# Small loads of rope tables and lambdas on POOL's queue, and another spread of the late modulation chunks

## The chip, the cores and the metric

The kernel runs on one core of a Trainium2 chip. The metric is the time of one execution on the device, in microseconds, as the median of several runs. Five engines of the core are named as in the profile: PE (matrix products; PEld is its weight load), DVE (vector), ACT (activations and copies), POOL (GpSimd) and SP (which here only issues DMAs). SPq, POOLq and so on are the engines' own instruction queues: they work in program order, and an instruction that waits holds what is queued behind it on the same engine.

## The reference, cut to what matters

One layer over 256 latent tokens and 256 context tokens of width 2048, all in fp32. A conditioning vector gives six modulation vectors of 2048 values. Attention and pooling run side by side, are merged by gates and projected; an MLP follows.

```python
mod = (jax.nn.silu(c) @ w_mod[l] + b_mod[l])[:, None, :]
sa, ca, ga, sm, cm, gm = jnp.split(mod, 6, axis=-1)
...
h_c = modulate(x_ctx, norm_attn_w[l], sa_c, ca_c)          # context: keys and values only
h = modulate(x, norm_attn_w[l], sa, ca)
p = h @ w_in[l]
q = axial_rope(rmsnorm(split_qk(p[..., Q_OFF:K_OFF]), q_norm_w[l]), row, col)
k = axial_rope(rmsnorm(split_qk(p[..., K_OFF:V_OFF]), k_norm_w[l]), row, col)
...
mix = token_mixer(q, k_all, v_all, p[..., P_OFF:G_OFF], p[..., G_OFF:], lam, ...)
x = x + ga * mix
x = x + gm * sq_relu_mlp(modulate(x, norm_mlp_w[l], sm, cm), w_ff1[l], w_ff2[l])
```

`token_mixer` holds a differential attention (8 heads, each the softmax of one pair of queries and keys minus `lam` times that of another), a pooling of the tokens in four groups with windows of 2, 4, 8 and 16, two up-projections, two sigmoid gates and the projection by `w_o`. `lam` is made from four small vectors, the lambdas. `ga`, `cm`, `sm` and `gm` are not needed before the projection and the MLP.

## The kernel before, in words

**The work.** All weights are fp32 in DRAM. They come in chunks of 128 x 1024 (512 KB), each into a tile `raw`. ACT casts a chunk to a high part `whi` (L245), DVE subtracts for a low part `wlo` (L246), and PE makes each product from high x high, high x low and low x high (`mm3`, L275 to 278; L454, L455 and L460 for the wide groups; L1028 and L1031 in the MLP). The high x low and high x high products come first, those with `wlo` last.

**The stages.** In order: the modulation of the attention norm (`w_m`, 16 steps f of 4 chunks, PE's `mod`) mixed with the first keys and queries; first values; second queries; second keys; second values; pooling (`w_p`, four groups); the gates and up-projections (`w_gb_in`, `w_b`, `w_ga_in`, `w_a`, four rounds); the projection (`w_o`); the MLP. Attention's scores run beside the second queries to the pooling: PE makes a block of scores, DVE its maximum (L687), ACT the exponential with the sum (L691), DVE the reciprocal and the factors (L694, L695, L697). ACT's exponential is the last reader of the scores' PSUM bank.

**Loads.** The list `stream` (from L127) names every load in its order, and SP issues them in this order a few chunks ahead of use (`load_next`, `wchunk` L255). Among the first loads stand two entries `prq`, at step 9 and step 11 of the modulation: three DMAs with rope tables and lambdas into tabs, wkt and wqt, then one more with the second pair of lambdas into a part of wqt. The last one overwrites columns that DVE still reads for the first pair of lambdas, so it waits for DVE. All four are issued in line L206.

**Late chunks.** `ga`, `cm`, `sm` and `gm` aren't made by PE. Each entry of `stream` has a `rate`, which its load adds to a credit (L248); each whole credit advances the generator `late_gen` (L597) by one. A vector has two halves, and a half takes 17 advances: one that clears the accumulator on POOL (L613) and loads the bias row (L614), and 16 that each issue the load of one chunk on SP and, one or two ticks later, one multiply-add on DVE over 128 x 1024 (`late_part`, L625). Behind the 16th of a half `late_fold` adds up the 128 partitions: seven DMAs that accumulate 64, 32, 16, 8, 4, 2 and 1 partitions onto the ones below (L630), all on POOL's queue, each waiting until the one before has landed; then one DMA to a row (L635; for `cm` L638 to L641) and one that spreads the row over the partitions (L642). Instructions that are not pinned (`pin`) are put in order on each engine by the language's scheduler, so that a clearing, a bias row or an addition on POOL can stand some way off its written place. The order of the names is fixed, so the rates decide in which stage the chunks of each lie.

**POOL's other work** around the change: for each group of pooling, `za` is cleared at its ends (L778, L779), ACT copies the PSUM into it (L780), POOL adds shifted copies (L785), and DVE finishes it (L796, L798, L800; `pool_diff` is placed some ticks later). For attention's norm POOL clamps the squares (L721) which PE sums (L725). In the MLP POOL squares the relu (L1039), ACT casts that (L272), and PE needs it for the next product.

Of the kernel before, what the change touches and what calls it, by code (L numbers as in the profile page):

```python
# [38 lines left out]
PRQ = {}  # L39
# [9 lines left out]
def layer(ctx: ExitStack, tc, a, out):  # L49
    nc = tc.nc  # L50
# [24 lines left out]
    def work(name, shape=None, dt=F32):  # L75
        return pool.tile(shape or [P, 512], dt, tag="w2", name=name, bufs=9)

    def s16(name, shape, dt=F32):
        return pool.tile(shape, dt, tag="s16", name=name, bufs=7)

    def s8(name, shape, dt=F32):
        return pool.tile(shape, dt, tag="s8", name=name, bufs=2)
# [32 lines left out]
    def raw_chunk(src, n=1024):  # L115
        raw = pool.tile([P, n], F32, tag="raw", name="raw", bufs=6)
        sp.dma_start(raw, src)
        return raw
# [9 lines left out]
    def plan(name, *idx, rate=0.0):  # L128
        stream.append(((name,) + idx, rate))
# [12 lines left out]
            plan("w_k", 0, f // 2)  # L142
            plan("w_q", 0, f // 2)
    FIRST_LOADS = len(stream)
    for n, g, rate in (("w_v", 0, 0.75), ("w_q", 1, 1.0), ("w_k", 1, 1.5), ("w_v", 1, 1.5)):
        for ch in range(8):
            plan(n, g, ch, rate=0.0 if (n, g) == ("w_v", 1) and ch < 3 else rate)
    for g in range(4):
        for i in range(4):
            plan("w_p", 2 * g + i // 2, i % 2, rate=0.5)  # L150
            if g > 1 and i == 1:
                plan("pool_w", g - 2)
    for g in range(4):
        for n, nk in (("w_gb_in", 8), ("w_b", 4), ("w_ga_in", 8), ("w_a", 4)):
            for ch in range(nk):
                plan(n, g, ch, rate=0.6)
                if g == 0 and n == "w_gb_in" and ch in (1, 7):
                    plan("pool_w", 2 if ch == 1 else 3)
    for g in range(4):
        for ch in range(8):  # L160
            plan("w_o", g, ch, rate=0.5 if g < 2 else 0.0)
            if ch % 4 == 0:
                plan("x", ch // 4, g)
    for b in range(9):
# [15 lines left out]
    def x1_tile():  # L180
        if not x1s:
            x1s.append(s16("x1", [P, 2, D]))
        return x1s[0]
# [5 lines left out]
    def mod_raw(f, i):  # L189

        home = f % 2 if f > 7 else f % 4
        if home == 0:
            return pool.tile([P, 1024], F32, tag="raw", name="raw", bufs=6)
        n = 2 if home == 1 else 4
        if i % n == 0:
            wide[0] = (s8 if home == 1 else s16)("raw", [P, n, 1024])
        return wide[0][:, i % n, :]

    def load_next():
        key, rate = stream[len(loaded)]  # L200
        src = a[key[0]]
        for i in key[1:] if key[0] != "prq" else ():
            src = src[i]
        if key[0] == "prq":
            for dst, names in prq[key[1]]:
                nc.sync.dma_start(dst, a["prq"][:, PRQ[names[0]][0]:PRQ[names[-1]][1]])  # L206
            loaded.append((key, None, None))
            return
        if key[0] in ("cT", "x"):
            dst = cT[:, 4 * key[1]:4 * key[1] + 4, :] if key[0] == "cT" else x1_tile()[:, key[1], key[2] * 512:key[2] * 512 + 512]  # L210
            nc.sync.dma_start(dst, src)
            loaded.append((key, None, None))
            return
        n = src.shape[-1]
        if key[0] == "w_m":
            raw = mod_raw(*key[1:])
            sp.dma_start(raw, src)
            loaded.append((key, raw, raw))
            return
        if key[0] in ("w_k", "w_q") and key[1] == 0:  # L220
            raw = pool.tile([P, n], F32, tag="aT", name="raw", bufs=2)
            sp.dma_start(raw, src)
            loaded.append((key, raw, raw))
            return
        raw = raw_chunk(src, n)
        if key == ("w_ff1a", 0):
            hi, lo = (pool.tile([P, n], F32R, tag="aT", name=nm, bufs=2) for nm in ("hi0", "lo0"))
        elif key == ("w_o", 3, 4):
            pair = s8("pair", [P, 2, 1024], F32R)
            hi, lo = pair[:, 0, :], pair[:, 1, :]  # L230
        elif key in (("w_ff1a", 2), ("w_ff1a", 3)):
            i = 2 * (key[1] - 2)
            if i == 0:
                early.append(s16("early", [P, 4, 1024], F32R))
            hi, lo = early[0][:, i, :], early[0][:, i + 1, :]
        elif key == ("w_ff1a", 1):
            halves = [[work(nm, dt=F32R) for nm in ("hi1", "lo1")] for _ in range(2)]
            for h in range(2):
                split(*halves[h], raw[:, h * 512:h * 512 + 512])
            loaded.append((key, *zip(*halves)))  # L240
            return
        else:
            hi = pool.tile([P, n], F32R, tag="whi", name="whi", bufs=3)
            lo = pool.tile([P, n], F32R, tag="wlo", name="wlo", bufs=3)
        act.copy(hi, raw)  # L245
        vec.tensor_sub(lo, raw, hi.bitcast(F32))  # L246
        loaded.append((key, hi, lo))
        credit[0] += rate if late[0] is not None else 0.0  # L248
        credit_rate[0] = rate
        while credit[0] >= 1.0:  # L250
            credit[0] -= 1.0
            if "gm" not in mods or mods["gm"] is not None or key[0] in ("w_ff1a", "w_ff1"):
                next(late[0], None)

    def wchunk(*key, ahead=AHEAD):  # L255
        while len(loaded) < min(done[0] + 1 + ahead, len(stream)) or loaded[done[0]][1] is None:
            if loaded and done[0] < len(loaded) and loaded[done[0]][1] is None:
                done[0] += 1
                continue
            load_next()  # L260
        got, hi, lo = loaded[done[0]]
        assert got == key, (got, key)
        loaded[done[0]] = None
        done[0] += 1
        tick()
        return hi, lo
# [4 lines left out]
    def split(hi, lo, src):  # L271
        act.copy(hi, src)  # L272
        vec.tensor_sub(lo, src, hi.bitcast(F32))
# [26 lines left out]
    def pr(name):  # L300
# [30 lines left out]
    prq = (((tabs[:, 2:4], ("cos", "sin")), (wkt, ("wk",)), (wqt, ("wq", "lq1", "lk1"))),  # L331
           ((wqt[:, 1:3], ("lq2", "lk2")),))
# [846 lines left out]
```

## Time and profile before

| | us |
|---|---|
| median of 3 runs | 1462.01 |
| lowest and highest run | 1460.66, 1462.44 |
| profiled execution, its own time | 1463.71 |
| its span | 1461.9 |
| mean granted clock of PE in it | 0.996 of full speed |

One execution was taken by the profiler, and all durations and waits come from it. A row of the timeline has the start in us, the duration (of several alike in a row: to the end of the last one), engine, line, operation, output and inputs, the count, and in brackets the idle time before it with what ended it. A row of the waits has the engine with the line that waited, the line and engine waited for, the total in us, how often, and the longest. A row of the windows has the stretch and its length, the busy time of PE, PEld, DVE, ACT and POOL with counts, and then the granted clock of PE, the share of the DMA engines' time, and GB/s. In the group of DMA issues a row ends in the size in KB and the us from issue to landing.

### The profile page before, as it was taken

What the parts mean: (1) busy time and instruction counts of PE and PEld (TensorE: products, weight loads), DVE (VectorE), ACT (ScalarE), POOL (GpSimd) and SP (SyncE); (2) the same over time, 40 slices, a digit from 0 to 9 for tenths busy, and PEclk for the clock granted to TensorE, in tenths of its full rate; (3) what the DMA queues carried; (4) which work ended last, traced back from release to release, by engine and by line L of the source; (5) the groups of instructions that cost most, each with busy time, mean ns of one, the idle gap of its engine ahead of it and who ended that gap; (6) DMA issues with size and microseconds to landing.
All of it is one profiled execution on the core that took longest, in us unless ns stands there. A gap on an engine that the chain in (4) does not pass through costs nothing.

```text
span 1461.9 us, 19786 instructions
## 1 busy us (share of the span) xinstructions
PE 1436.2 (98%) x7448; PEld 1182.0 (81%) x7448; DVE 990.7 (68%) x1218; ACT 669.3 (46%) x901; POOL 172.8 (12%) x194
## 2 busy tenths in 40 slices
PE   6999999999999999999999999999999999999998
PEld 4667887778888888888888888888888888888887
DVE  4557796858887777777767656666666465555675
ACT  5225335456654444444545545445344354544432
POOL 0001111104401010100001000011000110000260
PEclk9999999999999999999999999999999999999999
DMA  9997595445689999999746777787776665565563
GB/s 374 409 366 280 191 316 183 145 125 167 213 299 322 324 302 321 304 339 298 224 162 208 231 244 232 237 248 248 242 242 235 204 216 189 190 196 189 187 196 122
DMA packets 101328, 355.22 MB, mean 243 GB/s; under 512 B 12928, under 2 KB 13952, under 8 KB 101232
## 3 DMA queue, kind: packets, MB, share of 16 engines
q1 hardware_dynamic: 97200, 345.52, 69.5%
q0 software_dynamic: 4032, 8.44, 2.6%
q8 instruction: 58, 0.95, 0.3%
q14 instruction: 38, 0.31, 0.1%
HBM read 347.61 MB, written 2.13 MB: 239 GB/s over the span
## 4 chain that ended last, share of the span: by engine, by line
PE 84%; DMA 9%; DVE 4%; issue 1%; ACT 1%; POOL 0%; SPq 0%; DVEq 0%; ACTq 0%; POOLq 0%
PE f L1028 13%; PE f L455 8%; PE f L454 8%; PE f L460 8%; PE f L1031 7%; PE pg L454 4%; PE pg L455 4%; PE pg L460 4%; DMA raw<-in_w_m_dram 4%; DMA gm_bc<-gm_bc 2%; PE pyy L454 2%; PE pyy L455 2%; PE pyy L460 2%; PE wo L455 2%; PE wo L460 2%; PE wo L454 2%
## 5 line engine op out<-in xcount | busy, mean ns | idle before, releaser
L246 DVE TENSOR_TENSOR wlo<-raw,whi 128x1024 fp32r<-128x1024 f32 (+1 forms) x430 | 535.5, 1248 | 329.3 <-ACT whi L245 304.7
L245 ACT CAST whi<-raw 128x1024 fp32r<-128x1024 f32 (+1 forms) x430 | 449.8, 1048 | 547.2 <-PE f L455 184.5
L1028 PE MATMUL f<-h,whi 128*128 128x512 f32 x896 | 224.4, 393 | 1.0 <-ACT whi L245 1.0
L454 PE MATMUL f<-whi,act 128*128 128x512 f32 x512 | 199.4, 390 | 0.0
L455 PE MATMUL f<-whi,act 128*128 128x512 f32 x512 | 199.4, 389 | 0.0
L1028 PEld LDWEIGHTS f<-h,whi 128*128 128x128 f32 x896 | 161.7, 189 | 30.2 <-ACT whi L245 1.2
L460 PE MATMUL f<-wlo,act 128*128 128x512 f32 x512 | 136.9, 389 | 0.0
L1031 PEld LDWEIGHTS f<-h,wlo 128*128 128x128 f32 x896 | 122.3, 191 | 8.7
L1031 PE MATMUL f<-h,wlo 128*128 128x256 f32 x896 | 124.9, 283 | 0.0
L460 PEld LDWEIGHTS f<-wlo,act 128*128 128x128 f32 x512 | 96.1, 188 | 19.9
L454 PEld LDWEIGHTS f<-whi,act 128*128 128x128 f32 x512 | 96.1, 188 | 19.8
L455 PEld LDWEIGHTS f<-whi,act 128*128 128x128 f32 x512 | 96.2, 188 | 19.6
L454 PE MATMUL pg<-whi,hL 128*128 128x512 f32 x256 | 100.8, 394 | 0.0
L455 PE MATMUL pg<-whi,hL 128*128 128x512 f32 x256 | 99.7, 390 | 0.0
L625 DVE SCALAR_TENSOR_TENSOR sb<-raw,sil,sb 128x1024 f32<-128x1024 f32 x64 | 83.0, 1297 | 1.8 <-DMA sb<-in_b_cm_dram 1.8
L1039 POOL TENSOR_TENSOR rsq<-relu 128x512 f32<-128x512 f32 x28 | 29.2, 1042 | 427.3 <-ACT relu L1038 417.1
L460 PE MATMUL pg<-wlo,hL 128*128 128x512 f32 x256 | 68.5, 390 | 0.0
L454 PEld LDWEIGHTS pg<-whi,hL 128*128 128x128 f32 x256 | 48.1, 188 | 10.2 <-issue 0.2
L455 PEld LDWEIGHTS pg<-whi,hL 128*128 128x128 f32 x256 | 48.1, 188 | 10.0 <-issue 0.2
L460 PEld LDWEIGHTS pg<-wlo,hL 128*128 128x128 f32 x256 | 48.1, 188 | 10.0
L630 POOL DMA_DIRECT2D sb<-sb x28 | 22.4, 798 | 243.2 <-DVE sb L625 129.6
L1053 DVE TENSOR_TENSOR acc<-f,acc 128x512 f32<-128x512 f32 x48 | 30.9, 686 | 20.4 <-PE f L460 20.4
(280 smaller groups left out, 2185.4 us busy)
## 6 DMA issues: line engine op xcount, KB each, us to landing
raw<-in_w_ff_dram SPq DMA_DIRECT2D x240, 512.0 KB, 4.2
raw<-in_w_m_dram SPq DMA_DIRECT2D x64, 512.0 KB, 10.2
raw<-in_w_ga_dram SPq DMA_DIRECT2D x32, 512.0 KB, 4.6
raw<-in_w_cm_dram SPq DMA_DIRECT2D x32, 512.0 KB, 5.1
raw<-in_w_gb_in_dram SPq DMA_DIRECT2D x32, 512.0 KB, 4.7
raw<-in_w_ga_in_dram SPq DMA_DIRECT2D x32, 512.0 KB, 4.9
raw<-in_w_sm_dram SPq DMA_DIRECT2D x32, 512.0 KB, 5.4
raw<-in_w_o_dram SPq DMA_DIRECT2D x32, 512.0 KB, 4.7
```

The source lines that it names most:

```text
L245: act.copy(hi, raw)
L246: vec.tensor_sub(lo, raw, hi.bitcast(F32))
L454: pe.matmul(banks[t], tok(h, k, 0, tt), wt, start=k == 0, stop=False)
L455: pe.matmul(banks[t], tok(h, k, 1, tt), wt, start=False, stop=False)
L460: pe.matmul(banks[t], tok(h, k, 0, tt), wt, start=False, stop=k == 2 * nk - 1)
L625: pin(vec.scalar_tensor_tensor(o, raw, sil[:, 0, k:k + 1], o, ALU.mult, ALU.add))
L630: nc.gpsimd.dma_start(o[0:n, :], o[n:2 * n, :], accum_op=ALU.add)
L1028: pe.matmul(ps, hi[:, kk * P:kk * P + P], both(h2, k), start=k == 0, stop=False)
L1031: pe.matmul(ps[:, T:2 * T], lo[:, kk * P:kk * P + P], act_slice(h2, k, 0), start=False, stop=k == KT - 1)
L1039: gp.tensor_mul(sq, r, r)
L1053: vec.tensor_add(acc[:, t, gs], bs[t], acc[:, t, gs])
```

## The change

The four DMAs of line L206 are issued on POOL's queue. And the rates differ in six groups of loads: lower in second keys and second values, higher in pooling, gates and projection.

```diff
     FIRST_LOADS = len(stream)
-    for n, g, rate in (("w_v", 0, 0.75), ("w_q", 1, 1.0), ("w_k", 1, 1.5), ("w_v", 1, 1.5)):
+    for n, g, rate in (("w_v", 0, 0.75), ("w_q", 1, 1.0), ("w_k", 1, 1.0), ("w_v", 1, 0.75)):
         for ch in range(8):
             plan(n, g, ch, rate=0.0 if (n, g) == ("w_v", 1) and ch < 3 else rate)
     for g in range(4):
         for i in range(4):
-            plan("w_p", 2 * g + i // 2, i % 2, rate=0.5)
+            plan("w_p", 2 * g + i // 2, i % 2, rate=0.6)
...
             for ch in range(nk):
-                plan(n, g, ch, rate=0.6)
+                plan(n, g, ch, rate=0.63)
...
-            plan("w_o", g, ch, rate=0.5 if g < 2 else 0.0)
+            plan("w_o", g, ch, rate=0.6 if g < 2 else 0.0)
...
             for dst, names in prq[key[1]]:
-                nc.sync.dma_start(dst, a["prq"][:, PRQ[names[0]][0]:PRQ[names[-1]][1]])
+                nc.gpsimd.dma_start(dst, a["prq"][:, PRQ[names[0]][0]:PRQ[names[-1]][1]])
```

How the order of the instructions differs is shown at three places. An `x2` stands for two alike in a row.

On SP, in the modulation of the attention norm (before with −, after with +):

```order
-L217 DMA raw<-in_w_m_dram 128x1024
-L206 DMA tabs<-in_prq_dram 128x256
-L206 DMA wkt<-in_prq_dram 128x64
-L206 DMA wqt<-in_prq_dram 128x192
-L217 DMA raw<-in_w_m_dram 128x1024 x7
-L222 DMA raw<-in_w_k_dram 128x1024
-L222 DMA raw<-in_w_q_dram 128x1024
-L217 DMA raw<-in_w_m_dram 128x1024
-L206 DMA wqt<-in_prq_dram 128x128
-L217 DMA raw<-in_w_m_dram 128x1024 x7
```

The four L206 are gone from SP. They are now the first DMAs on POOL's queue, ahead of the first L613 (the clearing of ga_bc).

On DVE, in second values, between the last rope step L487 of the second keys and the next maxima L687; before:

```order
L694 RECIPROCAL rs<-sm_2344 128x2
L625 SCALAR_TENSOR_TENSOR ga_bc<-raw,sil,ga_bc 128x1024
L487 TENSOR_TENSOR qraw<-qraw,wkt 128x512
L695 TENSOR_TENSOR rs<-rs,lam_89 128x1
L246 TENSOR_TENSOR wlo<-raw,whi 128x1024
L697 SCALAR_TENSOR_TENSOR e<-e,rs 128x512
L625 SCALAR_TENSOR_TENSOR ga_bc<-raw,sil,ga_bc 128x1024 x2
L246 TENSOR_TENSOR wlo<-raw,whi 128x1024
L687 TENSOR_REDUCE mx<-sc 128x1 x2
```

And at the same place on DVE after the change:

```order
L694 RECIPROCAL rs<-sm_2331 128x2
L487 TENSOR_TENSOR qraw<-qraw,wkt 128x512
L695 TENSOR_TENSOR rs<-rs,lam_89 128x1
L246 TENSOR_TENSOR wlo<-raw,whi 128x1024
L697 SCALAR_TENSOR_TENSOR e<-e,rs 128x512
L246 TENSOR_TENSOR wlo<-raw,whi 128x1024
L687 TENSOR_REDUCE mx<-sc 128x1 x2
```

Three multiply-adds of late chunks are gone from this place; one stands behind the maxima, as before.

On POOL, from the second clearing of za for the last group of pooling to its additions; before:

```order
L785 TENSOR_TENSOR za<-za 128x265 x2
L778 MEMSET za 128x8
L779 MEMSET za 128x8
L778 MEMSET za 128x8
L779 MEMSET za 128x8
L785 TENSOR_TENSOR za<-za 128x271
L785 TENSOR_TENSOR za<-za 128x269
```

And on POOL after the change, from the accumulators of the next vector (sb), which are now cleared ahead of the third group's additions, to the clamp L721:

```order
L613 MEMSET sb 128x1024 x2
L785 TENSOR_TENSOR za<-za 128x271 x2
...
L614 DMA sb<-in_b_sm_dram 1x16x64
L630 DMA ga_bc<-ga_bc 64x1024
L614 DMA sb<-in_b_sm_dram 1x16x64
L630 DMA ga_bc<-ga_bc 32x1024
L630 DMA ga_bc<-ga_bc 16x1024
...
L630 DMA ga_bc<-ga_bc 8x1024
L785 TENSOR_TENSOR za<-za 128x271 x2
L785 TENSOR_TENSOR za<-za 128x269 x2
```

The fold of ga's second half, which stood ahead of the first group's additions, now stands around those of the last group: its first four DMAs ahead of the eight additions, three behind them, and then the clamp L721. The fold of sm's second half moves back in the same way, by some five chunks of the projection's loads.

## The prediction

> **What bounds the kernel now.** I read the page first, then the waits of PE, the waits of SP's DMA queue, the granted clock around the longest waits, and then the timeline of each place that the change touches. The profiled execution took 1463.7 us: the span below and 1.8 us around it. It is 1.7 us above the median of the three runs (1462.0). I work out a difference in the profiled execution and add it to the median.
>
> ```profile
> span 1461.9 us, 19786 instructions
> PE 1436.2 (98%) x7448; PEld 1182.0 (81%) x7448; DVE 990.7 (68%) x1218; ACT 669.3 (46%) x901; POOL 172.8 (12%) x194
> PE 84%; DMA 9%; DVE 4%; issue 1%; ACT 1%; POOL 0%; SPq 0%; DVEq 0%; ACTq 0%; POOLq 0%
> ```
>
> PE is the bound: busy for 98%, and 84% of the chain that ended last. An edit can only win back PE's idle time, or time at a lower clock; it loses what new idle time it makes. PE's waits, longest first:
>
> ```profile
> PE ssq L68 <- DVE sq L68: 10.6, 3, 6.9
> PE mod L68 <- DMA raw<-in_w_m_dram: 4.0, 6, 1.1
> PE qkT L492 <- ACT e L691: 2.6, 1, 2.6
> PE pin L278 <- DVE wlo L246: 1.3, 2, 1.0
> PE f L1028 <- ACT whi L245: 1.0, 1, 1.0
> ```
>
> The first row is the norm of the inputs and is not touched. The second and third are where the two parts of the change reach PE. Gates and projection are absent from the list: there PE waits for nothing that lasts. The clock fell in a stretch of 3.4 us right behind the second and the third wait:
>
> ```profile
> 97.40:100.80 3.40, 3.40 (x12) 2.72 (x9) 0.45 (x1) 0.00 (x0) 0.00 (x0) 0.50 1.03 420
> 278.30:281.70 3.40, 3.40 (x11) 2.76 (x10) 1.44 (x4) 1.73 (x5) 0.00 (x0) 0.51 0.87 287
> ```
>
> The last three columns are clock, DMA share and GB/s. Half clock for 3.4 us costs PE 1.7 us each time.
>
> **Part one, the rope tables and lambdas leave SP.** Four small DMAs leave SP's queue. Only the last of them waits: it overwrites columns of wqt that DVE still has to read.
>
> ```profile
> SPq L206 <- DVE wqt L68: 8.1, 1, 8.1
> ```
>
> ```profile
> 80.65 0.33 SPq L217 DMA_DIRECT2D raw<-in_w_m_dram  x1
> ```
>
> ```profile
> 89.66 0.33 SPq L206 DMA_DIRECT2D wqt<-in_prq_dram  x1
> 90.04 3.66 SPq L217 DMA_DIRECT2D raw<-in_w_m_dram  x7
> ```
>
> ```profile
> 95.11 0.64 PE L68 MATMUL mod<-raw,cv 128*32 128x256 f32 x8 [0.63 <-DMA raw<-in_w_m_dram]
> 96.86 0.64 PE L68 MATMUL mod<-raw,cv 128*32 128x256 f32 x8 [1.12 <-DMA raw<-in_w_m_dram]
> ```
>
> ```profile
> raw<-in_w_m_dram SPq DMA_DIRECT2D x64, 512.0 KB, 10.2
> ```
>
> SP issues nothing between 80.65 and 89.66. A load of this stage lands 10.2 us after its issue, so the one of 80.65 lands near 90.9, and in an unbroken train a load of 512 KB follows every 1.3 us (at the 420 GB/s above): the second at 93.5, the third at 94.8. PE, which has waited for them, starts on the second behind the stall at 95.11 and on the third at 96.86. The hole is 1.6 to 2.1 us, and PE shows it as 0.63 + 1.12 = 1.75. On POOL, the waiting DMA stands ahead of the memsets of ga_bc, more than 30 us later in the program, so nothing is held up there. The three that don't wait go to the very front of POOL's queue: the same 0.26 MB beside the first loads instead of beside later ones, a move of 0.7 us (0.26 MB at some 374 GB/s) that pays back later; I put it at nothing, and at most at 0.7 us lost. If only the hole goes, 1.7 us are won. If the half clock goes with it, 1.75 + 1.7 = 3.4 us could be, but then PE comes up against the train of loads, which itself moves by only 1.6 to 2.1 us. I take 2.6, the middle of the ends 1.7 and 3.4, since both rows count.
>
> The Trainium skill, "DMA: Bandwidth & Descriptors", section "Issuing engines are not separate DMA queues", speaks against this part: DMAs of all engines end on the same 16 DMA engines, and issuing on another one only saves issue time, which is small. By it this part is worth the 0.33 us of an issue row, and the sum below would be 2.3 us higher. The rows above show more than an issue: a wait in order that holds seven other loads; that is a rival below.
>
> **Part two, fewer late chunks in second keys and values.** Up to the end of second values the credits fall from 33.5 (8 × 0.75 + 8 × 1 + 8 × 1.5 + 5 × 1.5) to 25.75 (the last two now 8 × 1 and 5 × 0.75). Some eight late chunks move from there to pooling (8 to 9.6 credits), gates (57.6 to 60.5) and projection (8 to 9.6). In the DVE order shown in the section on the change, three multiply-adds L625 vanish between L694 and the pair L687.
>
> ```profile
> 272.64 2.59 DVE L625 SCALAR_TENSOR_TENSOR ga_bc<-raw,sil,ga_bc 128x1024 f32<-128x1024 f32 x2
> 275.15 1.22 DVE L246 TENSOR_TENSOR wlo<-raw,whi 128x1024 fp32r<-128x1024 f32 x1
> 276.28 1.28 DVE L687 TENSOR_REDUCE mx<-sc 128x1 f32<-128x512 f32 x2
> ```
>
> ```profile
> 277.00 0.69 ACT L691 ACTIVATE e<-sc,mx 128x512 f32<-128x512 f32 x1 [4.32 <-DVE mx L687]
> ```
>
> This is the whole of PE's 2.56 us: its transpose L492 needs the PSUM bank that ACT's exponential frees, the exponential needs the maximum, and the maximum stands behind two chunks on DVE. Without the 2.59 us the maximum ends at about 274.4, the exponential at about 275.7, and PE, which is there at 275.4, waits 0.3 to 0.4 instead of 2.56. The clock then has no reason to fall: 2.2 + 1.7 = 3.9 us won. Ends: 1.7 if a cast on ACT is next in line and holds the maximum up by half of it, 4.3 if the stall goes wholly. The eight moved chunks cost 8 × 1.3 = 10 us of DVE elsewhere, at nothing as far as gates and projection go, where PE waits for no DVE; if that cover is gone, one chunk costs at most its 1.3 us.
>
> The clock itself is weighed against the Trainium skill, "TensorE: Matmul & The Clock Gate", section "HAM oscillation — how this bites in real kernels": gaps of PE should stay below about 3.4 us. Here half clock followed an idle time of 2.56 us, and another one of 0.63 and 1.12 us, but not the 1.03 us of L278; the trace is stricter than the rule. By the rule alone, the 1.7 us behind the 2.56 us wouldn't depend on that wait, and the sum would be 1.7 us higher.
>
> **What part two brings in: the fold of ga.** The second half of ga is full at the end of pooling instead of the end of second values. Behind its last chunk come seven accumulating DMAs on POOL's queue, each waiting for the one before to land. POOL executes in order, and in the order shown the first four of them now stand ahead of the last eight additions L785 of pooling. Before, the fold was over by then. Two other folds give its pace and its load:
>
> ```profile
> 311.29 0.91 POOL L630 DMA_DIRECT2D ga_bc<-ga_bc  x1 [19.80 <-DVE rs L695]
> ...
> 325.69 0.79 POOL L630 DMA_DIRECT2D ga_bc<-ga_bc  x1 [2.38 <-DMA ga_bc<-ga_bc]
> ...
> 329.89 2.13 POOL L613 MEMSET sb<- 128x1024 f32 x2
> ```
>
> ```profile
> 435.35 0.92 POOL L630 DMA_DIRECT2D sb<-sb  x1 [36.02 <-DVE sb L625]
> ...
> 454.91 0.79 POOL L630 DMA_DIRECT2D sb<-sb  x1 [4.03 <-DMA sb<-sb]
> ```
>
> ```profile
> 311.30:325.70 14.40, 14.40 (x87) 11.16 (x86) 7.80 (x12) 9.64 (x16) 2.46 (x4) 1.00 0.47 110
> 380.00:400.00 20.00, 20.00 (x117) 17.82 (x116) 19.13 (x25) 10.50 (x17) 9.84 (x13) 1.00 0.69 218
> 435.40:454.90 19.50, 19.50 (x87) 16.16 (x87) 12.86 (x11) 8.82 (x10) 2.41 (x3) 1.00 1.00 337
> ```
>
> From the first to the fourth DMA it is 14.4 us where 110 GB/s flow and 19.6 where 337. At the 218 GB/s of 380 to 400 the line between them gives 14.4 + 108 / 227 × 5.2 = 16.8.
>
> ```profile
> 373.69 3.91 POOL L785 TENSOR_TENSOR za<-za 128x271 f32<-128x271 f32 x6 [0.87 <-ACT za L780]
> ```
>
> ```profile
> 385.76 7.90 POOL L785 TENSOR_TENSOR za<-za 128x271 f32<-128x271 f32 x8 [1.53 <-ACT za L780]
> 397.36 1.96 POOL L721 TENSOR_SCALAR osq<-osq 128x512 f32<-128x512 f32 x1 [3.69 <-ACT osq L720]
> ```
>
> ```profile
> 393.70 0.17 DVE L798 TENSOR_TENSOR za<-za,prm 128x7 f32<-128x7 f32 x1 [0.83 <-POOL za L785]
> 393.81 1.23 DVE L246 TENSOR_TENSOR wlo<-raw,whi 128x1024 fp32r<-128x1024 f32 x1
> ```
>
> ```profile
> 397.28 1.07 PE L460 MATMUL pg<-wlo,hL 128*128 128x512 f32 x4
> ```
>
> On the clock of before: the six additions of the third window end at 377.6; the two memsets that now stand ahead of them (2.1 us for two, 0.7 of them in POOL's idle time) move that to 379.0, which also lets PE's 1.03 us at L278 grow by up to 1.4. A bias row's issue comes next (0.5), so the fold starts at 379.6, its fourth DMA is issued at 396.4, which takes POOL until 397.2. The eight additions last 5.2 us at 0.65 each, as the six took (7.9 as in before). So they end at 402.4; then DVE's L798 (0.2) and L246 (1.2) and PE's L460 starts at 403.9 instead of 397.28: 6.6 us lost, the growth at L278 within it. PE stands still for some 5.2 us, so the clock falls behind it: another 1.7 as in the rows above. Ends: 4 (a fold in 14.4 us, and no clock loss) and 12 (19.6 us, additions in 7.9, half clock for two stretches less what PE catches up). I take 6.6 + 1.7 = 8.3. The square's clamp L721, behind three more steps of the fold, ends near 413, and its reader on PE moves with PE's loss to 414: nothing, at most 1.6.
>
> **The later folds.** Those of cm and sm move by a few chunks; sm's ends some 14 us later than 710, over 15 us ahead of its first use:
>
> ```profile
> 709.78 0.58 POOL L642 DMA_DIRECT2D sb<-row  x1 [2.20 <-DMA row<-sb]
> ```
>
> ```profile
> L922 DVE SCALAR_TENSOR_TENSOR yt<-yt,rq_y,sb x16: 477/479/486, 742.8 to 781.3; 128x256 f32<-128x256 f32 x16
> ```
>
> In the MLP the fold of gm that ended before POOL's L1039 at 1168 held PE for 1.0 us (last row of PE's waits). It starts a chunk, 2.7 us, earlier, but L1039 now stands one step further down it: 0.8 won, between 1.0 won and 3 lost.
>
> **The sum.** −2.6 − 3.9 − 0.8 + 8.3 = +1.0 us. On the median: 1462.0 + 1.0 = 1463.0.
>
> **The rivals.**
>
> A. The fold doesn't bind: its steps land faster than at 311, or PE has slack that I don't see. For it: DVE had a slack of 2.2 us there (L246 done at 395.04, used at 397.28). Against it: none of the stretches above was under 14.4 us to the fourth step, and 6.6 us are to be covered. The gains stand, less the 1.4 at L278: 1462.0 − 7.3 + 1.4 = 1456.1. Chance 0.23.
>
> B, the other side. The fold at its slow pace. From 16.8 us on every us more is PE's own. With 19.6 us (as at 435, DMA at its full share), additions at 7.9 and the L721 wait of 1.6, the loss is 8.3 + 2.8 + 2.7 + 1.6 = 15.4 at the far end; half way, 11.9: 1462.0 − 7.3 + 11.9 = 1466.6. It decides slower where these come to 1.9 us more than I took, so from a fold of 18.7 us. For it: DVE is busy 19.1 of 20 us there, so it has no reserve once it was held. Against it: the load is 218 GB/s. Chance 0.20.
>
> C. The first part brings nothing, since the transfers bind that stage and the seven delayed ones only burst (3.66 us for seven issues): 1463.0 + 2.6 = 1465.6. Against it: PE's two waits fit the hole. The page on DMA says this one. Chance 0.08.
>
> D. The clock is not won back at 278, since its cause lies elsewhere: 1463.0 + 1.7 = 1464.7, in the band of no change. The page on the clock says this one. Chance 0.05.
>
> **How the numbers follow.** The forecast has the other 0.44, with 1459 to 1466 as its own range from the ends of the terms. A measurement of this kernel can tell some 0.2% (2.9 us) from no change. Faster: A, and 0.06 of the forecast, 0.29. Slower: B, C and 0.03 of the forecast, 0.31. The rest, 0.40, is within. The range reaches to A's 1456 and into B, to 1468.
>
> **What would show it.** In the profile after: no wait of SP at L206, PE's waits for in_w_m down to some 2 us, clock 1.0 at 97 and 278; L492 waiting under 0.5; a new wait of PE at L460 for L246, of DVE at L798 for L785 of 5 us or more, with four L630 of ga_bc ahead of eight L785 on POOL between 379 and 398, all of it some 6 us earlier for what is won ahead. I am wrong if that wait at L460 is missing (A), if it is over 8 us (B), or if 97 and 278 still show half clock (C, D).

## The result, and the profile after

The changed kernel takes 1463.85 us (median of 12 runs, 1462.18 to 1466.99), the kernel before, measured anew, 1461.51 (12 runs, 1459.34 to 1463.21). The ratio is 1.0019, with a 95% interval of 1.0010 to 1.0028: slower by 1.5 to 4.1 us, where 1.0 us was forecast. The profiled execution of after took 1466.99 us, 3.3 more than that of before; it is the slowest of the 12 runs.

The page of the profile after, and PE's waits in it:

```profile
span 1465.2 us, 19771 instructions
PE 1437.8 (98%) x7448; PEld 1182.7 (81%) x7448; DVE 989.2 (68%) x1218; ACT 671.4 (46%) x901; POOL 175.1 (12%) x198
```

```profile
PE ssq L68 <- DVE sq L68: 10.9, 3, 7.0
PE pin L278 <- DVE wlo L246: 3.5, 1, 3.5
PE f L1028 <- ACT whi L245: 2.7, 1, 2.7
PE mod L68 <- DMA raw<-in_w_m_dram: 2.2, 5, 0.6
PE pg L460 <- DVE wlo L246: 1.2, 1, 1.2
PE modT L68 <- DVE blocks L68: 1.0, 1, 1.0
PE qkT L492 <- ACT e L691: 0.5, 1, 0.5
```

Both gains are there: the waits for in_w_m fell from 4.0 to 2.2 us, L492 from 2.6 to 0.5, and SP has no wait at L206. Three waits grew or are new: L278 from 1.3 to 3.5, L1028 from 1.0 to 2.7, L460 from nothing to 1.2.

The granted clock (third column from the end) in three stretches of after:

```profile
374.00:377.40 3.40, 2.79 (x13) 2.79 (x14) 3.37 (x7) 0.00 (x0) 1.14 (x2) 0.50 0.70 78
377.40:380.70 3.30, 3.30 (x17) 3.30 (x17) 2.89 (x7) 1.66 (x2) 0.79 (x1) 0.50 1.00 382
1172.60:1176.00 3.40, 2.79 (x7) 2.21 (x8) 3.15 (x5) 2.99 (x5) 0.00 (x0) 0.50 0.24 52
```

The half clock at 97 and 278 us is gone. Two stretches in a row from 374 and one at 1172 have come, behind the grown waits at L278 and L1028.

POOL's timeline of after around the last group of pooling:

```profile
366.93 1.83 POOL L613 MEMSET sb<- 128x1024 f32 x2
368.73 4.46 POOL L785 TENSOR_TENSOR za<-za 128x271 f32<-128x271 f32 x6
373.14 0.57 POOL L614 DMA_DIRECT2D sb<-in_b_sm_dram  x1
373.71 0.92 POOL L630 DMA_DIRECT2D ga_bc<-ga_bc  x1
...
389.74 0.82 POOL L630 DMA_DIRECT2D ga_bc<-ga_bc  x1 [3.52 <-DMA ga_bc<-ga_bc]
390.29 5.24 POOL L785 TENSOR_TENSOR za<-za 128x271 f32<-128x271 f32 x8
395.22 1.05 POOL L630 DMA_DIRECT2D ga_bc<-ga_bc  x1
```

And who waited for it, first on DVE, then on PE:

```profile
394.87 0.86 DVE L798 TENSOR_TENSOR za<-za,prm 128x7 f32<-128x7 f32 x2 [8.08 <-POOL za L785]
395.67 2.36 DVE L246 TENSOR_TENSOR wlo<-raw,whi 128x1024 fp32r<-128x1024 f32 x2
```

```profile
396.95 1.20 PE L460 MATMUL pg<-wlo,hL 128*128 128x512 f32 x4 [1.25 <-DVE wlo L246]
```

This chain runs as the prediction drew it: four DMAs of the fold, then the eight additions, then L798, L246 and L460. From the first to the fourth DMA it is 16.0 us (16.8 forecast), and the additions last 5.24 (5.2). DVE's wait at L798 is 8.1 us, where 5 or more were forecast. PE had been 7.0 us ahead of before (the L455 that starts at 281.81 there, at the end of the half clock, starts at 274.78 here); now L460 starts at 396.95 against 397.28.

POOL in the MLP of after, the second fold of gm:

```profile
1132.09 0.87 POOL L630 DMA_DIRECT2D gm_bc<-gm_bc  x1 [23.88 <-DVE gm_bc L625]
...
1168.04 0.53 POOL L635 DMA_DIRECT2D row<-gm_bc  x1 [3.06 <-DMA gm_bc<-gm_bc]
1169.92 0.56 POOL L642 DMA_DIRECT2D gm_bc<-row  x1 [1.36 <-DMA row<-gm_bc]
1170.50 1.06 POOL L1039 TENSOR_TENSOR rsq<-relu 128x512 f32<-128x512 f32 x1
```

The same fold in before:

```profile
1134.20 0.87 POOL L630 DMA_DIRECT2D gm_bc<-gm_bc  x1 [26.59 <-DVE gm_bc L625]
...
1167.63 0.52 POOL L635 DMA_DIRECT2D row<-gm_bc  x1 [3.15 <-DMA gm_bc<-gm_bc]
1168.16 1.06 POOL L1039 TENSOR_TENSOR rsq<-relu 128x512 f32<-128x512 f32 x1
```

The fold starts earlier than before (1132.09 against 1134.20), but L1039 starts later (1170.50 against 1168.16), and PE stands at L1028 for 2.7 us.

### The profile page after: what moved, and what is told of

Its sections match the earlier page's. It is cut to its first block, busy times and chain, and to the rows that moved or that the text cites. A ratio compares the mean times of both kernels' runs of the same rounds, so it can differ in the third digit from the quotient of the medians.

```text
span 1465.2 us, 19771 instructions
## 1 busy us (share of the span) xinstructions
PE 1437.8 (98%) x7448; PEld 1182.7 (81%) x7448; DVE 989.2 (68%) x1218; ACT 671.4 (46%) x901; POOL 175.1 (12%) x198
## 4 chain that ended last, share of the span: by engine, by line
PE 83%; DMA 11%; DVE 2%; issue 2%; POOL 1%; ACT 1%; SPq 0%; DVEq 0%; ACTq 0%; POOLq 0%
PE f L1028 13%; PE f L455 8%; PE f L454 8%; PE f L460 8%; PE f L1031 7%; DMA raw<-in_w_m_dram 6%; PE pg L460 4%; PE pg L454 4%; PE pg L455 4%; DMA gm_bc<-gm_bc 2%; PE pyy L460 2%; PE v L455 2%; PE v L454 2%; PE pyy L454 2%; PE pyy L455 2%; PE v L460 2%
## 5 line engine op out<-in xcount | busy, mean ns | idle before, releaser
L246 DVE TENSOR_TENSOR wlo<-raw,whi 128x1024 fp32r<-128x1024 f32 (+1 forms) x430 | 536.9, 1251 | 334.2 <-ACT whi L245 307.9
L1028 PE MATMUL f<-h,whi 128*128 128x512 f32 x896 | 225.7, 394 | 2.7 <-ACT whi L245 2.7
L455 PE MATMUL f<-whi,act 128*128 128x512 f32 x512 | 199.3, 389 | 0.0
L1028 PEld LDWEIGHTS f<-h,whi 128*128 128x128 f32 x896 | 162.5, 190 | 32.4 <-ACT whi L245 2.9
L460 PE MATMUL f<-wlo,act 128*128 128x512 f32 x512 | 136.8, 389 | 0.0
L460 PEld LDWEIGHTS f<-wlo,act 128*128 128x128 f32 x512 | 96.1, 188 | 19.9
L455 PEld LDWEIGHTS f<-whi,act 128*128 128x128 f32 x512 | 96.2, 188 | 19.8
L455 PE MATMUL pg<-whi,hL 128*128 128x512 f32 x256 | 99.7, 389 | 0.0
L625 DVE SCALAR_TENSOR_TENSOR sb<-raw,sil,sb 128x1024 f32<-128x1024 f32 x64 | 81.9, 1280 | 0.1
L1039 POOL TENSOR_TENSOR rsq<-relu 128x512 f32<-128x512 f32 x28 | 29.1, 1041 | 435.0 <-ACT relu L1038 424.8
L460 PE MATMUL pg<-wlo,hL 128*128 128x512 f32 x256 | 68.6, 390 | 1.2 <-DVE wlo L246 1.2
L460 PEld LDWEIGHTS pg<-wlo,hL 128*128 128x128 f32 x256 | 48.0, 188 | 11.6 <-DVE wlo L246 1.7
L455 PEld LDWEIGHTS pg<-whi,hL 128*128 128x128 f32 x256 | 48.1, 188 | 10.1 <-issue 0.2
```

Source lines behind the costliest of these rows:

```text
L455: pe.matmul(banks[t], tok(h, k, 1, tt), wt, start=False, stop=False)
L460: pe.matmul(banks[t], tok(h, k, 0, tt), wt, start=False, stop=k == 2 * nk - 1)
L625: pin(vec.scalar_tensor_tensor(o, raw, sil[:, 0, k:k + 1], o, ALU.mult, ALU.add))
L1028: pe.matmul(ps, hi[:, kk * P:kk * P + P], both(h2, k), start=k == 0, stop=False)
L1039: gp.tensor_mul(sq, r, r)
```

## The experiments

All times are medians, with the ratio to the kernel before on the same chip and its 95% interval. The ratio is not taken from the two medians, so a gain in us by the one and by the other can differ by about 1 us. The runs of before that they are compared with have medians of 1461.4 to 1461.9 us.

**One: only the small loads.** The kernel before with this edit alone:

```diff
-                nc.sync.dma_start(dst, a["prq"][:, PRQ[names[0]][0]:PRQ[names[-1]][1]])
+                nc.gpsimd.dma_start(dst, a["prq"][:, PRQ[names[0]][0]:PRQ[names[-1]][1]])
```

> The kernel before with the four small loads on POOL's queue and no other edit. Theory: the hole in the train of loads and the half clock at 97 us go, worth 3.5 us (PE's lag in the trace after moves by that much between 93 and 102 us): 3 to 4 us faster than before, SP without a wait at L206, clock 1.0 at 97 us, the half clock at about 275 us still there. Rival (the loads bind that stage and only burst): 0 to 1 us, PE's waits for in_w_m move elsewhere in the stage.

Measured: 1457.19 us, ratio 0.9973 (0.9963 to 0.9984), so 0.0027 × 1461.7 = 3.9 us faster (2.3 to 5.4 by the interval; 4.5 by the medians). PE's waits:

```profile
PE qkT L492 <- ACT e L691: 2.6, 1, 2.6
PE mod L68 <- DMA raw<-in_w_m_dram: 1.8, 5, 0.6
```

The waits for in_w_m are 1.8 instead of 4.0, SP has no wait at L206, the clock at 97 us is 1.00, and the theory stands against the rival. One detail of it is wrong: L492 still waits 2.6 us, but no half clock follows it.

```profile
272.00:276.00 4.00, 2.71 (x14) 2.36 (x15) 2.91 (x6) 3.04 (x7) 0.00 (x0) 1.00 0.91 317
```

**Two: only the rates.** The changed kernel with the four small loads back on SP (the diff above the other way round).

> The changed kernel with the four small loads back on SP. Theory (the two parts add up): 3 to 4 us slower than the changed kernel, so 5 to 7 us slower than before, with half clock at 97 us. Rival (the parts share one gain, or the gain of the small loads is lost later anyway): within 1.5 us of the changed kernel, 1 to 4 us slower than before.

Measured: 1467.97 us, ratio 1.0050 (1.0038 to 1.0062), 4.1 us above the changed kernel. The two parts add up. The half clock that was expected at 97 us is not there: in this profile the granted clock is 1.00 from 97.4 to 101, so it is the hole itself that came back here. PE waits at it for 0.63 and 0.93 us (0.38 in after), and the same product of PE starts 1.7 us later than in after behind the hole (96.46 against 94.72) and 2.9 us later by 111 (110.67 against 107.79).

**Three: the fold of ga behind pooling's additions.**

```diff
-            plan("w_p", 2 * g + i // 2, i % 2, rate=0.6)
+            plan("w_p", 2 * g + i // 2, i % 2, rate=0.5)
...
-                plan(n, g, ch, rate=0.63)
+                plan(n, g, ch, rate=0.647)
```

> The changed kernel with the rate in pooling back at 0.5 and 0.647 in place of 0.63 in gates, so that the credits at the MLP are nearly the same: the whole fold of ga's second half now stands behind pooling's additions on POOL. Theory (the fold and the clearings ahead of the additions cost 7.6 us): 5 to 7.6 us faster than the changed kernel, so 3 to 5 us faster than before, no wait of DVE at L798 over 4 us, no half clock at 374 us, while the wait at 1170 us stays. Rival (the loss between 370 and 400 us comes from the additional late chunks on DVE): within 2 us of the changed kernel, since as many chunks lie in pooling and gates.

Measured: 1456.12 us, ratio 0.9970 (0.9959 to 0.9981), so by the medians 5.6 us faster than before and 7.7 us faster than the changed kernel (4.4 and 7.2 by the ratios). POOL's timeline, and PE's waits:

```profile
377.39 7.91 POOL L785 TENSOR_TENSOR za<-za 128x271 f32<-128x271 f32 x8 [1.53 <-ACT za L780]
385.23 0.87 POOL L630 DMA_DIRECT2D ga_bc<-ga_bc  x1
```

```profile
PE osum L725 <- POOL osq L721: 1.7, 1, 1.7
PE f L1028 <- ACT whi L245: 1.5, 1, 1.5
...
PE pin L278 <- DVE wlo L246: 0.3, 1, 0.3
```

With the fold behind the additions, L460 doesn't wait at all and L278 0.3 us. As many late chunks lie in pooling and gates together as in the changed kernel, and from 365 to 400 us DVE even does five multiply-adds L625 here against three there, so DVE's share of them isn't the cause: the rival falls. The edit moves the clearings along with the fold, so the 7.7 us are those of both; six takes them apart. PE now waits at L725 for the clamp L721, which stands behind three DMAs of the fold.

**Four: the chunks of gm two loads earlier.**

```diff
-            plan("w_o", g, ch, rate=0.6 if g < 2 else 0.0)
+            plan("w_o", g, ch, rate=0.63 if g < 2 else 0.0)
```

> The changed kernel with 0.63 in place of 0.6 in the projection: the chunks of gm come two loads (5.5 us) earlier in the MLP, the rest nearly stays. Theory (POOL's fold of gm holds L1039 and so PE at 1170 us): the fold ends some 4 us ahead of L1039, PE's wait for whi at L1028 and the half clock behind it go, 3 to 4 us faster than the changed kernel, so about 1 us faster than before. Rival (that wait comes from ACT or from the loads and not from the fold): the wait stays within 1 us and the time within 1 us of the changed kernel.

Measured: 1462.45 us, ratio 1.0010 (1.0001 to 1.0018), an interval that overlaps that of the changed kernel (1.0010 to 1.0028). POOL in the MLP:

```profile
1163.78 0.56 POOL L642 DMA_DIRECT2D gm_bc<-row  x1 [3.65 <-DMA row<-gm_bc]
1164.35 1.06 POOL L1039 TENSOR_TENSOR rsq<-relu 128x512 f32<-128x512 f32 x1
```

PE has no wait at L1028 left in this profile, so the fold of gm is the cause. L1039 still stands right behind L642, not 4 us behind it as expected, but it starts 6.2 us earlier than in after. The time fell by 1.4 us and not by 3 to 4, and the kernel stays slower than before, not faster: the forecast had counted the half clock of one profile as if every execution had it.

**Five: the same on top of three.** Rates 0.5 in pooling, 0.647 in gates, 0.62 in the projection.

> The kernel with the fold behind pooling's additions (rates 0.5, 0.647) and 0.62 in the projection, so that the chunks of gm come two loads earlier. Theory (the fold of gm holds L1039): the 1.5 us that PE still waits at L1028 for whi go, 1 to 2 us faster than with 0.6 and 6 to 8 us faster than before; the osum wait of 1.7 us stays. Rival (ACT or the loads set that wait): it stays over 1 us, time within 0.7 us of that with 0.6.

Measured: 1454.60 us, ratio 0.9958 (0.9944 to 0.9972). That is 1.5 us below three, as expected; the wait at L1028 is gone, the one at L725 is 1.9. Half clock follows it in this profile (from 399.8 to 403.2), as it did not follow the 1.7 us of three.

**Six: the clamp ahead of the fold.** Rates 0.3, 0.68 and 0.63.

> As the one before, with 0.3 in pooling, 0.68 in gates and 0.63 in the projection: on POOL the clamp L721 now stands ahead of the whole fold of ga. Theory: the osum wait of 1.7 us goes too, so 1 to 2 us faster than the kernel with 0.5, 7.5 to 9.5 us faster than before. Rival (a fuller DMA in gates, 0.68 against 0.647 late chunks per load, makes PE wait for weights there): no gain or a loss against the kernel with 0.5, new waits of PE at L454 to L460 between 400 and 650 us.

Measured: 1456.84 us, ratio 0.9969 (0.9957 to 0.9981): no gain on three and a loss on five. The wait at L725 is gone as expected, but not for the rival's reason is there no gain. PE's longest wait in that stretch, and POOL's rows ahead of it:

```profile
PE pin L278 <- DVE wlo L246: 2.3, 1, 2.3
```

```profile
364.63 1.83 POOL L613 MEMSET sb<- 128x1024 f32 x2
366.43 3.59 POOL L785 TENSOR_TENSOR za<-za 128x271 f32<-128x271 f32 x6
```

Here the scheduler put two clearings between the clamp and the third group's additions, as in the changed kernel, and no fold is near. L278 waits 2.3 us against 0.3 in three, where they stood elsewhere, and the clock from 372.1 to 375.5 is 0.50. So the miss shows apart what the clearings alone cost at L278: 2.0 us of waiting.

**Seven and eight: a second profile of after and of before**, with no edit.

> The changed kernel once more, for a second profile. Theory (whether an idle time of PE below 3.4 us costs clock depends on where it falls against a grid of 3.4 us that starts anew in every execution): the waits of PE at L278, L460 and L1028 come again within 1 us of the first profile, but the half clock behind them differs in place or length, and the span with it, by 1.7 us for each stretch. Rival (half clock follows from the wait alone): half clock again from 374 to 381 and at 1173 us.

> The kernel before once more, for a second profile. Theory (the grid starts anew): the waits at 95, 97 and 275 us come again, with half clock behind none, one or two of them, and a span of 1458 to 1462 us. Rival: half clock again at 97 and 278 us, span within 0.5 us of the first.

After, again (span 1465.4 us): L278 3.5, L460 2.8 and L1028 2.7 us. The clock behind the three:

```profile
374.30:377.70 3.40, 3.11 (x14) 3.11 (x15) 3.37 (x8) 0.00 (x0) 0.81 (x2) 0.50 0.78 110
377.70:381.10 3.40, 3.40 (x31) 3.40 (x30) 3.40 (x6) 1.67 (x2) 0.79 (x1) 1.00 1.01 395
398.20:401.60 3.40, 3.40 (x9) 2.64 (x8) 3.40 (x5) 0.04 (x1) 0.77 (x1) 0.50 0.84 280
1172.60:1176.00 3.40, 1.33 (x6) 1.11 (x7) 2.04 (x3) 2.94 (x5) 0.42 (x1) 1.00 0.49 154
```

Before, again (span 1459.1 us): L492 waits 2.6 us and in_w_m 3.9, as in the first profile, and behind both the clock is full.

```profile
97.50:101.00 3.50, 3.50 (x17) 2.80 (x15) 0.01 (x1) 0.00 (x0) 0.00 (x0) 1.00 1.02 415
276.00:280.00 4.00, 3.07 (x16) 2.64 (x17) 2.75 (x5) 3.03 (x7) 0.00 (x0) 1.00 0.94 323
```

The waits come again, L460's not within the 1 us that was expected (2.8 against 1.2). The half clock doesn't come where it was: at 374 one stretch instead of two, a new one at 398, none at 1172, and in before none at 97 and 278. The two spans of before differ by 2.8 us, nearly the 3.4 of its two stretches; those of after by only 0.2, though the second has one stretch less: it waits 1.6 us longer at L460, time that the second stretch of the first profile took up. The sum of the waits for in_w_m is 3.7 in the second profile of after, no lower than in before; but its waits lie elsewhere, and at the hole, from 94 to 97 us, it has 0.43 and before again 0.60 + 1.58.

Half clock doesn't follow from the wait alone. What it follows can be worked out from the profiles. In each of them the changes of the clock lie whole multiples of 3.413 us apart (in before at 97.43, 278.34 and 281.75: 53 and 1 of them; in after at 373.90, 380.73 and 1172.62: 2 and 232), and the place of this grid differs from execution to execution. Cells of the grid around L492, first in before (the wait lies in one cell), then in before again (it lies across two):

```profile
274.93:278.34 3.41, 0.85 (x7) 0.45 (x6) 3.41 (x5) 1.34 (x4) 0.00 (x0) 1.00 0.93 332
278.34:281.75 3.41, 3.41 (x10) 2.77 (x9) 1.40 (x4) 1.69 (x5) 0.00 (x0) 0.50 0.87 286
```

```profile
272.61:276.02 3.41, 1.76 (x11) 0.88 (x7) 3.37 (x5) 0.01 (x1) 0.00 (x0) 1.00 0.90 285
276.02:279.43 3.41, 2.50 (x13) 2.19 (x14) 2.33 (x5) 3.02 (x7) 0.00 (x0) 1.00 0.96 340
```

And the cells around L1028, first in after, then in after again:

```profile
1169.21:1172.62 3.41, 1.29 (x10) 1.05 (x8) 0.38 (x1) 1.03 (x2) 1.62 (x2) 1.00 0.38 133
```

```profile
1169.58:1172.99 3.41, 2.37 (x15) 1.92 (x13) 0.00 (x0) 0.00 (x0) 2.04 (x3) 1.00 0.09 16
1172.99:1176.40 3.41, 1.73 (x8) 1.43 (x9) 2.44 (x4) 3.34 (x5) 0.03 (x1) 1.00 0.41 139
```

Over all eleven profiles, without the first 36 and the last 6 us, each of the nine cells in which PE was idle for 1.9 us or more is followed by half clock. Of those with less than 1.7 us none is, but for one: the second stretch of after, from 377, follows a cell with 0.7 us of idle time that itself ran at half clock. Two lie between: 1.74 us at 94 in before is followed by it, 1.84 at 271 in one is not.

**Nine: clearings and clamps both out of the way.** Rates 0.35, 0.66 and 0.64.

> The changed kernel with 0.35 in pooling, 0.66 in gates and 0.64 in the projection. On POOL both pairs of clearings L613 now stand ahead of the clamp L721 that precedes the third group's additions, and the last clamp ahead of the whole fold of ga. Theory (two clearings between a clamp and the additions cost 2.0 us at L278, a fold ahead of the last clamp 1.9 us at L725, gm's fold 1.5 to 2.7 us at L1028): none of the three waits is over 0.6 us, 8 to 10 us faster than before, 1 to 3 us faster than the kernels with 0.5 or 0.3 in pooling. Rival (these waits are replaced by others of DVE or the loads in that stretch): within 1 us of the kernel with 0.5 (0.996 of before), and PE's idle time between 365 and 425 us stays at 2 us or more.

Measured: 1453.73 us, ratio 0.9946 (0.9932 to 0.9959), 7.9 us faster than before by the ratio (7.7 by the medians), just short of the forecast 8 to 10, and the best of all. PE's waits:

```profile
PE ssq L68 <- DVE sq L68: 10.9, 2, 7.1
PE mod L68 <- DMA raw<-in_w_m_dram: 2.5, 5, 0.7
PE wo L68 <- ACT whi L245: 1.9, 1, 1.9
...
PE qkT L492 <- ACT e L691: 0.5, 1, 0.5
```

L278, L460, L725 and L1028 are gone from the list. Between 365 and 425 us the profile shows no idle time of PE, where five has 2.2 us, so the rival falls. The gain on five is 0.9 us by the medians, and the two intervals overlap, so it is at the edge of what can be told; a new wait of 1.9 us in the last step of the projection takes part of the gain, and its cause wasn't tried.

## Why the prediction was right, point by point

**The small loads**: right in mechanism, a little small. 2.6 us were forecast, 3.9 (2.3 to 5.4 by the interval) measured alone in one, and 4.1 between two and the changed kernel. The hole alone was 1.6 to 2.2 us of PE's waits in the three profiles that have it, and 0.4 to 0.5 in both of after and in that of one. The clock, which the forecast took in for a part, isn't what makes up the rest: half clock stood behind the hole in one of the three profiles only, and two is 2.9 us behind after by 111 us without it.

**The three chunks ahead of the maxima**: the stall was right (2.2 us forecast; 2.6 to 0.5 is 2.1). The 1.7 us of clock on top were counted as certain, and were only there in one of the three profiles that have this wait (not in before again, not in one). On the median the term was not measured alone: it lies between 2.1 and 3.8.

**The fold of ga**: the size was right, 8.3 forecast and 7.7 between three and the changed kernel. (Three also waits 1.7 us at L725, which the changed kernel doesn't, and 1.2 us less at L1028.) The chain came to L460 as worked out: forecast 403.9 on before's clock, less the 7.0 us that PE was ahead, is 396.9; measured 396.95. Its parts lay elsewhere. The step that failed is that the growth at L278 would be up to 1.4 and L460's wait some 5: two clearings cost 2.0 us there (six), the six additions took 4.46 instead of 3.91, L278 waited 3.5, and half clock behind it used up most of what PE would have waited at L460, where only 1.2 to 2.8 us remained. The half clock was so in part inside the 6.6 us and not on top of them.

**The fold of gm**: wrong. The step "it starts a chunk, 2.7 us, earlier, but L1039 now stands one step further down it: 0.8 won" failed. The fold did start 2.1 us earlier, but from its first DMA to L1039 it took 38.4 us instead of 34.0: L642 and the wait for the row ahead of it cost some 2, and from the first DMA to L635 it took 2.5 us longer. The same order took 36.7 us in two, where L1028 waited 1.0, and 38.4 in the second profile of after. Against the 1.0 us of before the term is so a loss of 0 to 1.7 us in waiting, plus clock where it falls. Shifting the fold by two loads gave 1.4 us on the changed kernel and 1.5 on three, but that takes away the whole wait and not only what was added.

**The sum**: −3.9 − 2.1 + 7.7 = +1.7, up to 1.7 lower where the clock behind L492 is won back, and 0 to 1.7 higher for the fold of gm. Measured are 2.3 between the medians, and 1.0 were forecast. There is luck in a number this close: the first two terms were off in opposite ways, by 1.3 and up to 1.8, the fold of ga by 0.6, and the fold of gm had the wrong sign. What moved the sum off +1.0 can't be told from terms this uncertain; the fold of gm is the only one with the wrong sign. Of the rivals, A (the fold doesn't bind) and C (the small loads bring nothing) are refuted by three and one. B's slow fold did not come: to its fourth DMA it took 16.0 us in after, 15.8 in two and 16.3 in after again, the pace that the forecast took. D was half right: the clock behind L492 isn't bound to that wait in every execution.

The rule of the Trainium skill, "TensorE: Matmul & The Clock Gate", section "HAM oscillation — how this bites in real kernels" (no gaps of PE above about 3.4 us), fits no better than the forecast's: half clock followed 2.56 us of idle time in one profile of before and not 2.6 in the other, and it followed 2.3 us in six. What tells them apart is how much of the idle time falls into one cell of the grid (eight).

## What to carry to other kernels

When work is spread differently over stages, ask first where the tail of each unit lands: here three multiply-adds ahead of a maximum cost 2.1 us and the others nothing that shows, while the chain of seven DMAs behind the last one, with its clearings, cost 7.7 us, since they stood on an in-order queue ahead of short work that others waited for. Look also at the small things that a scheduler moves along: two clearings of 0.9 us ahead of six additions made PE wait 2 us longer. And take a half clock seen in one profile for a chance, not for a term: where a wait falls on the grid differs in each execution.

## What the runs showed of the hardware

Half clock came in whole cells of a grid of 3.413 us, which lies elsewhere in each execution. It followed all nine cells in which PE was idle for 1.9 us or more, and none with less than 1.7 that ran at full clock itself. So the same wait was followed by it in one execution and not in another: in before 2.56 us with and 2.6 without, in after 2.7 at L1028 with (first profile) and without (second). The 3.5 us at L278 were followed by it in all four profiles that have them (after twice, two and four), for one or two stretches of 3.4 us. So part of the scatter of single runs (4.8 us over the 12 of after) can be of this kind, and one profile can't price it.
